# A two-layer encoder on one core: two projections in 512-column blocks, a new order of the projection stage, and three smaller moves

## The chip, the cores and the metric

The kernel runs on one core of a Trainium2 chip. The metric is device time in microseconds (us); lower is better. A core has five engines that run their own instruction streams and wait for one another on semaphores: PE (TensorE, matrix products), DVE (VectorE), ACT (ScalarE), POOL (GpSimd) and SP (SyncE, which here issues all DMA transfers). PE writes its results to PSUM; this kernel divides PSUM into seven shared banks of 128x512 values and one more for sums.

## The reference

Two equal layers work on x of 2048 tokens by 1024 features, in float32.

```
h    = rmsnorm(x, pre_g)
proj = h @ W_in                        # 1024 x 2816
u_a, v_a, g_a, q, k, v, g_b = split(proj, [512, 512, 512, 512, 128, 128, 512])
# group A, chunks of 128 positions, 8 channel groups of 64
z    = W_s (128x128 per group) @ layernorm(v_a) + b
y_a  = u_a * z * silu(g_a)
# group B, 8 query heads, 2 kv heads, head size 64, all tokens attend to all
q, k = axial_rope(rmsnorm(q)), axial_rope(rmsnorm(k))
y_b  = softmax(q k^T / 8) v * silu(g_b)
out  = concat(y_a, y_b) @ W_out
x    = x + rmsnorm(out, post_g)
```

## The kernel before

**Precision.** A projection multiplies in three passes: each operand is split into a high part (rounded to the matrix engine's float32 form) and a low rest, and high x high, high x low and low x high are added up in PSUM. With 8 slices of 128 features, one output tile takes 24 matmuls. Weights are loaded as `w_raw`, then split: ACT copies the high part `w_hi`, DVE subtracts to get `w_lo` (L268), in pieces of 128x1024 values.

**Stages.** A layer has a projection stage and an attention stage. The projection stage runs over two halves; a half has two groups of 512 tokens, a group four token tiles of 128. `hT` holds a group's normalised, transposed activations. For each half `run` goes, weight block by weight block, over both groups:

1. keys and values (`do_kv`), and the first four query heads (`do_q`, block 0);
2. Q1, the last four query heads (`do_q`, block 1);
3. VA, the mixed values v_a: two blocks of 256 columns into one PSUM bank, then `do_va`: layer norm on DVE (L424 to L429), a split by ACT and POOL (`fl`, L436), and 16 "mixes" per group, each three matmuls with the spatial weights `ws` and two DVE steps into `fb` with the bias `zbias` (L448), the result stored to `z_d`;
4. GB, the second gate g_b: two blocks of 256 columns, a tanh on ACT, one DVE step (L476), a store to `gb_d`;
5. the first gate and u_a, four times 128 + 128 columns (`do_gate`), here with the weights as the stationary operand and 512 activations streaming (`proj_ch`).

With tokens as the stationary operand (`proj_tok`), a matmul streams 256 weight columns. `norm_rope` is the work on a group of queries: squares on ACT, a sum (L351), a reciprocal root by ten small steps, a multiply (L358), t1 on POOL (L360), t2 on DVE (L363) and their sum `fc` (L365); PE then transposes `fc` and the result goes to `q_d`.

**Order.** PE's instructions stand in program order. Work that has to be slipped in between projections (transposes, mixes, the first row maxima) is put in a list `bg` with a delay in ticks; a tick is 8 matmuls of 256 columns or 4 of 512, and takes up to two due jobs. `spatial_weights` makes the transposed weights `wsT` and `zbias` in such jobs. The other engines' instructions in the projection stage are ordered by a scheduler; in the attention stage they stand in program order too. SP issues its DMAs in order, and an issue that waits holds all behind it.

**Row maxima.** Attention needs the row maximum of every score before the softmax. They come from a separate cheap product: for one unit (a group and a head) 16 matmuls `pmax` from `q_m`, each followed by a DVE maximum into `mx` (L683), then `m_neg` over four of them (`max_row`), then `stack_max`, in which PE transposes m_neg and the rows go to `m_d`. The first eight units run as jobs during GB and the first gate in the layer's second half (`last_jobs`, after `scale_v`, which finds the values' maximum); the others during attention, spread over its key tiles.

**Attention.** For each unit, 16 key tiles of 128: two matmuls `sp`, two exponentials on ACT (`p_parts`, `p_f`), a subtraction on POOL or DVE (`p_parts`), products `po` and `sums`. Between them PE does the output product `pout` of the group before (`fill`). Behind each finished token tile a list `post_queue` holds small steps: a reciprocal root, two adds `o_t`, a store, and in layer 0 also a norm for the next layer. In each key tile the loop takes steps from it; when a last part begins, the queue is emptied at once.

Of the kernel before, what the change touches and what calls it, by code (L numbers as in the profile page):

```python
# [9 lines left out]
F32 = mybir.dt.float32  # L10
# [9 lines left out]
P = 128  # L20
# [5 lines left out]
HD = 64  # L26
# [12 lines left out]
def encoder(ctx: ExitStack, tc, x, w_in, w_out, pre_g, post_g, ln_a_g, ln_a_b,  # L39
# [31 lines left out]
    def ps_t(name):  # L71
        return psum.tile([P, GRP], F32, name=name, tag="ps", bufs=7)
# [102 lines left out]
    class Project:  # L175
# [39 lines left out]
        def spatial_weights(self):  # L215
            l = self.l
            self.lng = lay.tile([P, 4], F32, name="lng")
            nc.sync.dma_start(self.lng, ln_a_g[l].rearrange("(t p) -> p t", p=P))
            self.zbias = lay.tile([P, 4, P], F32, name="zbias")
            wsT = row_t("wsT")  # L220
            for hf in range(2):
                raw = f_t("fa")
                nc.sync.dma_start(raw.rearrange("p (g j) -> p g j", g=4),
                                  spatial_w[l, 4 * hf:4 * hf + 4].rearrange("g i j -> i g j"))
                hi = f_t("fh", dt=F32R)
                lo = f_t("fl", dt=F32R)

                def t(hf=hf, raw=raw, hi=hi, lo=lo):
                    ps = ps_t("pt")
                    for g in range(4):  # L230
                        PE.transpose(ps[:, g * P:(g + 1) * P], raw[:, g * P:(g + 1) * P], ident)
                    sl = slice(hf * GRP, (hf + 1) * GRP)
                    nc.vector.tensor_copy(wsT[:, sl], ps)
                    nc.scalar.copy(hi, wsT[:, sl])
                    nc.gpsimd.tensor_tensor(lo, wsT[:, sl], hi.bitcast(F32), ALU.subtract)
                    nc.sync.dma_start(ws_d[:, 0, sl], hi.bitcast(F32))
                    nc.sync.dma_start(ws_d[:, 1, sl], lo.bitcast(F32))
                bg.add(WS_DELAY + 2 * hf, t)
            lnb = f_t("fb")
            nc.sync.dma_start(lnb, ln_a_b[l].partition_broadcast(P))  # L240
            sb = row_t("sb_row", (1, D))
            nc.sync.dma_start(sb, spatial_b[l:l + 1].rearrange("o g i -> o (g i)"))
            for c in range(4):
                def b(c=c):
                    ps = ps_t("pt")
                    PE.matmul(ps[:, 0:2 * P], lnb[:, c * P:(c + 1) * P], wsT[:, 2 * c * P:(2 * c + 2) * P],
                              start=True, stop=False)
                    PE.matmul(ps[:, 0:2 * P], ones1, sb[:, 2 * c * P:(2 * c + 2) * P], start=False, stop=True)
                    nc.vector.tensor_copy(self.zbias[0:HD, c, :], ps[0:HD, 0:P])
                    nc.vector.tensor_copy(self.zbias[HD:P, c, :], ps[HD:P, P:2 * P])  # L250
                bg.add(WS_DELAY + 8 + 2 * c, b)

        def load_w(self, cols):
# [7 lines left out]
        def split_w(self, raw, n=4):  # L261

            hi = w_t([P, ND, WB], "w_hi")
            lo = w_t([P, ND, WB], "w_lo")
            for d in range(0, ND, n):
                sl = slice(d, d + n)
                nc.scalar.copy(hi[:, sl], raw[:, sl])  # L267
                nc.vector.tensor_tensor(lo[:, sl], raw[:, sl], hi.bitcast(F32)[:, sl], ALU.subtract)  # L268
            return hi, lo

        def hT_jobs(self, g, tail=False):

# [41 lines left out]
        def proj_tok(self, hT, j, w, ps=None, c0=0):  # L314
            if ps is None:
                ps = ps_t("pp")
            n = 0
            for a, b in PASSES:
                for d in range(ND):
                    PE.matmul(ps[:, c0:c0 + WB], hT[d // 4][:, a, d % 4, j * P:(j + 1) * P], w[b][:, d, :],  # L320
                              start=(n == 0), stop=(n == 3 * ND - 1))
                    n += 1
                bg.tick()
            return ps

        def proj_ch(self, hT, w, c0):
# [142 lines left out]
            nc.sync.dma_start(y_d[g][:, c, 0], hi.bitcast(F32))  # L469
            nc.sync.dma_start(y_d[g][:, c, 1], lo.bitcast(F32))  # L470

        def do_gb(self, g, banks, b):
            for i, ps in enumerate(banks):
                th = f_t("fa")
                nc.scalar.activation(th, ps, AF.Tanh, scale=0.5)
                nc.vector.scalar_tensor_tensor(th, th, 1.0, ps, ALU.add, ALU.mult)  # L476
                nc.sync.dma_start(gb_d[g][:, 2 * i:2 * i + 2, b * WB:(b + 1) * WB],
                                  th.rearrange("p (t e) -> p t e", t=2))

        def scale_v(self):  # L480

# [39 lines left out]
        def run(self, kv, first, last_jobs, first_wo):  # L521
# [5 lines left out]
            for n, gs in enumerate(halves):  # L527
# [13 lines left out]
                for i, g in enumerate(gs):  # L541
                    if i == 0:
                        for f in self.stores:
                            f()
                        self.stores = []
                    if i == len(gs) - 1:
                        raw = self.load_w([C_Q + WB])
                    self.do_kv(g, self.banked(hTs[g], w_kv))
                    if i == len(gs) - 1:
                        w_next = self.split_w(raw)  # L550
                        raw = self.load_w([C_VA])
                    self.do_q(g, self.banked(hTs[g], w), 0)
                if n == 0:
                    self.spatial_weights()
                w = w_next
                for i, g in enumerate(gs):
                    self.do_q(g, self.banked(hTs[g], w), 1)
                    if i == 0:
                        w_next = self.split_w(raw)
                w = w_next  # L560
                raw = self.load_w([C_VA + WB])
# [3 lines left out]
                w = [w, self.split_w(raw)]  # L565
                raw = self.load_w([C_GB])
                for g in gs:
                    vs = []
                    for j in range(TPG):
                        ps = self.proj_tok(hTs[g], j, w[0])  # L570
                        self.proj_tok(hTs[g], j, w[1], ps, WB)
                        v = f_t("fv")
                        nc.scalar.copy(v, ps)
                        vs.append(v)
                    self.do_va(g, vs, ws)
                w = self.split_w(raw)
                blocks = [[C_GB + WB]] + [[C_GA + c * P, C_U + c * P] for c in range(4)]
# [5 lines left out]
                for b in range(2):  # L583
                    raw = self.load_w(blocks.pop(0))
                    for i, g in enumerate(gs):
                        self.do_gb(g, self.banked(hTs[g], w), b)
                        if i == 0:
                            w_next = self.split_w(raw)
                    w = w_next
# [39 lines left out]
    def attend(l, kv, nxt):  # L629
# [25 lines left out]
        def at(k, f):  # L655
            later.setdefault(k, []).append(f)
# [33 lines left out]
        def stack_max(u, pe, act, dve):  # L690
            s = state[u]
            qb, h = units[u]
            ps = ps_t("t2")
            pe.transpose(ps[0:TPG, 0:P], s.m, ident)
            for i in range(2):
                rows = small.tile([TPG, P], F16, name="m_rows", bufs=4)
                if i == 0:
                    hi = rows
                    act.activation(rows, ps[0:TPG, 0:P], AF.Copy, bias=EXP_SHIFT)
                else:  # L700
                    dve.scalar_tensor_tensor(rows, ps[0:TPG, 0:P], EXP_SHIFT, hi, ALU.add, ALU.subtract)
                nc.sync.dma_start(m_d[qb][h, i].rearrange("(t p) -> t p", p=P), rows)
# [341 lines left out]
        for u in range(pre, len(units)):  # L1044
            k0 = (u - pre) * span
            if k0 >= 8:
                at(k0 - 8, lambda u=u: load_qm(u))
            for n in range(steps):
                at(k0 + n * span // steps, lambda u=u, n=n: max_step(u, n, PE, DVE))
            at(k0 + span + 1, lambda u=u: max_row(u, DVE))  # L1050
            at(k0 + span + 3, lambda u=u: stack_max(u, PE, ACT, DVE))

        def load_gb(u):
            qb, h = units[u]
# [37 lines left out]
        for k in range(end + 4):  # L1092
            if k < total:
# [10 lines left out]
                ACT.activation(p_f(k), sp, AF.Exp)  # L1104
                if not dve_share(k):
                    sub_lo(k, POOL)
            for _ in range(2):
                if post_queue:
                    post_queue.pop(0)()
            kb = k - 1  # L1110
            if 0 <= kb < total and dve_share(kb):
                sub_lo(kb, DVE)
# [119 lines left out]
```

## Time and profile before

| | |
|---|---|
| median of 3 runs | 2775.79 us (2775.23 to 2775.82) |
| profiled execution | 2771.47 us, of it 2769.3 us span |
| projection and attention, layer 0 | about 0 to 629 and 629 to 1382 us |
| projection and attention, layer 1 | about 1382 to 1992 and 1992 to 2769 us |
| PE busy in these four stretches | 595, 736, 597, 749 us |
| DVE busy in them | 461, 496, 452, 488 us |
| mean granted clock of PE | 0.992 |

How to read it: the page gives busy time and count of each engine; records of matmuls overlap, so the mean of one (290 ns at 256 columns) is longer than the distance to the next. A group's row ends with the idle time ahead of its instructions and what released them; a row of waits has total, times and longest; a timeline row has the start, the length of a run of equal instructions with their number, and in brackets the idle time before it. A row of a window has, after the window and its length, busy time and count of PE, PEld (the weight loads), DVE, ACT and POOL, then the granted clock, the DMA share and GB/s. Nearly all instructions of the attention stage, and PE's everywhere, carry L84, the line of a helper, so they are told apart by tile names.

### The profile page before, as it was taken

What the parts mean: (1) busy time and instruction counts of PE and PEld (TensorE: products, weight loads), DVE (VectorE), ACT (ScalarE), POOL (GpSimd) and SP (SyncE); (2) the same over time, 40 slices, a digit from 0 to 9 for tenths busy, and PEclk for the clock granted to TensorE, in tenths of its full rate; (3) what the DMA queues carried; (4) which work ended last, traced back from release to release, by engine and by line L of the source; (5) the groups of instructions that cost most, each with busy time, mean ns of one, the idle gap of its engine ahead of it and who ended that gap; (6) DMA issues with size and microseconds to landing.
All of it is one profiled execution on the core that took longest, in us unless ns stands there. A gap on an engine that the chain in (4) does not pass through costs nothing.

```text
span 2769.3 us, 48428 instructions
## 1 busy us (share of the span) xinstructions
PE 2677.1 (97%) x18230; PEld 1782.0 (64%) x18230; DVE 1896.8 (68%) x3796; ACT 1522.7 (55%) x3005; POOL 1287.0 (46%) x1080
## 2 busy tenths in 40 slices
PE   7999999999999999999999999999999999999997
PEld 6898899764444444444589989997644444444444
DVE  8862688876666776776487528888766666666664
ACT  4221432117887787787732214221288877778774
POOL 1210122007786676776632101210277767667765
PEclk9999999999999999999999999999999999999999
DMA  4424522322222232222354334333322222221313
GB/s 143 146 81 127 165 76 81 112 63 89 89 71 81 75 98 79 82 80 80 110 179 138 115 114 134 88 92 98 94 64 72 82 70 73 81 76 47 112 46 129
DMA packets 275310, 265.31 MB, mean 96 GB/s; under 512 B 19202, under 2 KB 233346, under 8 KB 275076
## 3 DMA queue, kind: packets, MB, share of 16 engines
q1 hardware_dynamic: 275076, 262.22, 30.2%
q8 instruction: 143, 2.34, 0.3%
q14 instruction: 91, 0.75, 0.1%
HBM read 177.09 MB, written 85.07 MB: 95 GB/s over the span
## 4 chain that ended last, share of the span: by engine, by line
PE 77%; DVE 11%; ACT 5%; DMA 3%; issue 2%; POOL 1%; SPq 0%; DVEq 0%; POOLq 0%; ACTq 0%
PE pp L84 27%; PE sp L84 14%; PE po L84 11%; PE pout L84 11%; PE pmax L84 7%; PE sums L84 4%; PE pt L84 2%; DVE fc L363 2%; ACT p_parts L84 2%; ACT p_f L84 2%; DMA w_raw<-in_w_in_dram 1%; DVE mx L84 1%; DVE o_t L84 1%; DVE w_lo L268 1%; ACT w_hi L267 1%
## 5 line engine op out<-in xcount | busy, mean ns | idle before, releaser
L84 POOL TENSOR_TENSOR p_parts<-p_f,p_parts 128x512 f16<-128x512 f32 x872 | 1034.9, 1205 | 404.2 <-ACT p_f L84 304.3
L84 ACT ACTIVATE p_parts<-sp 128x512 f16<-128x512 f32 x1024 | 630.0, 615 | 296.5 <-PE sp L84 289.8
L84 DVE TENSOR_REDUCE mx<-pmax 128x1 f32<-128x512 f32 x768 | 513.0, 681 | 211.9 <-PE pmax L84 209.9
L84 PE MATMUL pout<-wo,y_t 128*128 128x512 f32 x1488 | 657.1, 506 | 0.7 <-ACT p_f L84 0.3
L84 PE MATMUL po<-p_parts,v_st 128*32 128x512 f16 (+1 forms) x3072 | 639.2, 383 | 0.2
L84 ACT ACTIVATE p_f<-sp 128x512 f32<-128x512 f32 x1024 | 632.0, 617 | 0.0
L84 PE MATMUL pp<-w_hi,hT 128*128 128x256 f32 x3584 | 502.5, 290 | 16.1 <-DVE hT L310 9.7
L84 PEld LDWEIGHTS pp<-w_hi,hT 128*128 128x128 f32 x3584 | 462.0, 194 | 21.8 <-DVE hT L310 10.9
L84 PE MATMUL sp<-q_st,k_t 128*128 128x512 f16 x1024 | 390.2, 381 | 8.3 <-DVE mx L84 5.5
L84 PE MATMUL pmax<-k_t,q_m 128*128 128x512 f16 x1024 | 389.7, 382 | 7.6 <-DVE mx L84 3.2
L84 PEld LDWEIGHTS <-v_st 128*32 128x32 f16 (+1 forms) x3072 | 193.7, 96 | 309.5 <-issue 253.0
L84 PE MATMUL sp<-q,k_t 66*128 66x512 f16 x1024 | 391.0, 382 | 0.0
L84 PEld LDWEIGHTS pout<-wo,y_t 128*128 128x128 f32 x1488 | 281.3, 190 | 128.4 <-issue 8.7
L84 PEld LDWEIGHTS <-k_t 128*128 128x128 f16 (+1 forms) x2048 | 191.5, 99 | 187.7 <-issue 74.4
L468 POOL TENSOR_TENSOR fl<-fa,fh 128x512 fp32r<-128x512 f32 x32 | 43.1, 1346 | 533.3 <-ACT fh L467 489.2
L84 PE MATMUL pp<-hT,w_hi 128*128 128x512 f32 x1024 | 271.7, 413 | 0.0
L84 PE MATMUL pp<-w_lo,hT 128*128 128x256 f32 x1792 | 262.6, 290 | 0.0
L84 PE MATMUL sums<-p_parts,one_h 128*32 128x512 f16 x2048 | 242.3, 380 | 0.0
L84 PEld LDWEIGHTS pp<-w_lo,hT 128*128 128x128 f32 x1792 | 235.5, 194 | 0.9
L84 PEld LDWEIGHTS pp<-hT,w_hi 128*128 128x128 f32 x1024 | 193.4, 190 | 35.3
L683 DVE TENSOR_REDUCE mx<-pmax 128x1 f32<-128x512 f32 x256 | 172.6, 687 | 49.1 <-PE pmax L84 47.5
L84 PEld LDWEIGHTS <-q_m 128*128 128x128 f16 x1024 | 99.8, 98 | 140.2 <-issue 42.1
(161 smaller groups left out, 2790.9 us busy)
## 6 DMA issues: line engine op xcount, KB each, us to landing
w_raw<-in_w_in_dram SPq DMA_DIRECT2D x28, 1024.0 KB
y_t<-y_d SPq DMA_DIRECT2D x56, 512.0 KB
w_raw<-in_w_in_dram SPq DMA_DIRECT2D x32, 512.0 KB
x_t<-in_x_dram SPq DMA_DIRECT2D x16, 512.0 KB
z_d<-fb SPq DMA_DIRECT2D x32, 256.0 KB
gb_d<-fa SPq DMA_DIRECT2D x32, 256.0 KB
fb<-z_d SPq DMA_DIRECT2D x32, 256.0 KB
y_d<-fh SPq DMA_DIRECT2D x32, 256.0 KB
```

The lines of the kernel that those rows point to most:

```text
L84: return tc.keep_in_program_order(call(*args, **kw))
L267: nc.scalar.copy(hi[:, sl], raw[:, sl])
L268: nc.vector.tensor_tensor(lo[:, sl], raw[:, sl], hi.bitcast(F32)[:, sl], ALU.subtract)
L363: nc.vector.tensor_tensor(t2[:, :, :, lo:lo + 16], qn[:, :, :, hi:hi + 16], tbi[:, :, 1:2, lo:lo + 16].broadcast_to([P, 2, n, 16]), ALU.mult)
L468: nc.gpsimd.tensor_tensor(lo, th, hi.bitcast(F32), ALU.subtract)
L683: dve.tensor_reduce(s.mx[:, j, c:c + 1], ps, AX.X, ALU.max)
```

## The change

The layer's order becomes: keys and first queries, VA, Q1, GB, first gate. VA and GB use weights of 512 columns: `load_wide` loads two tiles of four feature slices each, `split_wide` splits them on ACT and DVE, and `proj_wide` multiplies 512 columns at once, with a tick every 4 matmuls. `do_gb` now stores one token tile at a time. `spatial_weights` is called ahead of the first group's queries, not after both groups'; its copies out of PSUM move from DVE to ACT. The second half of a 256-column weight block's low part is made on GpSimd. In attention `stack_max` comes two key tiles later, and the loop takes one step from `post_queue` in a key tile, not two.

```diff
 spatial_weights:
-                    nc.vector.tensor_copy(wsT[:, sl], ps)
+                    nc.scalar.copy(wsT[:, sl], ps)
...
-                    nc.vector.tensor_copy(self.zbias[0:HD, c, :], ps[0:HD, 0:P])
-                    nc.vector.tensor_copy(self.zbias[HD:P, c, :], ps[HD:P, P:2 * P])
+                    nc.scalar.copy(self.zbias[0:HD, c, :], ps[0:HD, 0:P])
+                    nc.scalar.copy(self.zbias[HD:P, c, :], ps[HD:P, P:2 * P])
 split_w:
-                nc.vector.tensor_tensor(lo[:, sl], raw[:, sl], hi.bitcast(F32)[:, sl], ALU.subtract)
+                engine = nc.gpsimd if n == 4 and d else nc.vector
+                engine.tensor_tensor(lo[:, sl], raw[:, sl], hi.bitcast(F32)[:, sl], ALU.subtract)
+        def load_wide(self, c):
+            raws = [w_t([P, ND // 2, 2 * WB], "w_raw", F32) for _ in range(2)]
+            for q, raw in enumerate(raws):
+                nc.sync.dma_start(raw, w_in[self.l, q * GRP:(q + 1) * GRP, c:c + 2 * WB]
+                                  .rearrange("(d p) e -> p d e", p=P))
+            return raws
+        def split_wide(self, raws):
+            parts = [], []
+            for raw in raws:
+                hi, lo = [w_t([P, ND // 2, 2 * WB], name) for name in ("w_hi", "w_lo")]
+                for d in range(0, ND // 2, 2):
+                    sl = slice(d, d + 2)
+                    nc.scalar.copy(hi[:, sl], raw[:, sl])
+                    nc.vector.tensor_tensor(lo[:, sl], raw[:, sl], hi.bitcast(F32)[:, sl], ALU.subtract)
...
+        def proj_wide(self, hT, j, w):
+            ps = ps_t("pp")
+            n = 0
+            for a, b in PASSES:
+                for d in range(ND):
+                    PE.matmul(ps, hT[d // 4][:, a, d % 4, j * P:(j + 1) * P], w[b][d // 4][:, d % 4, :],
+                              start=(n == 0), stop=(n == 3 * ND - 1))
+                    n += 1
+                    if n % 4 == 0:
+                        bg.tick()
+            return ps
 do_gb:
-                nc.sync.dma_start(gb_d[g][:, 2 * i:2 * i + 2, b * WB:(b + 1) * WB],
-                                  th.rearrange("p (t e) -> p t e", t=2))
+            nc.sync.dma_start(gb_d[g][:, j], th)
 run, order of a half:
+                    if n == 0 and i == 0:
+                        self.spatial_weights()
...
-                for i, g in enumerate(gs):
-                    self.do_q(g, self.banked(hTs[g], w), 1)
...
-                        ps = self.proj_tok(hTs[g], j, w[0])
-                        self.proj_tok(hTs[g], j, w[1], ps, WB)
+                        ps = self.proj_wide(hTs[g], j, w)
...
+                    if i == 0:
+                        w_next = self.split_w(raw)
+                w = w_next
+                raws = self.load_wide(C_GB)
+                for i, g in enumerate(gs):
+                    self.do_q(g, self.banked(hTs[g], w), 1)
+                    if i == 0:
+                        w_next = self.split_wide(raws)
...
+                for i, g in enumerate(gs):
+                    for j in range(TPG):
+                        self.do_gb(g, j, self.proj_wide(hTs[g], j, w))
 attend:
-            at(k0 + span + 3, lambda u=u: stack_max(u, PE, ACT, DVE))
+            at(k0 + span + 5, lambda u=u: stack_max(u, PE, ACT, DVE))
...
-            for _ in range(2):
-                if post_queue:
-                    post_queue.pop(0)()
+            if post_queue:
+                post_queue.pop(0)()
```

Three pieces of the engines' order show what moves; the line numbers behind the change are those of the changed file. First DVE in layer 0's second half, from the last norm of the values to the first maxima `mx`. Before (`rs_y`, `rs_t` are the reciprocal root, `fv` the normed values):

```order
L448 SCALAR_TENSOR_TENSOR fb<-pt,lng,zbias 64x128
L124 SCALAR_TENSOR_TENSOR rs_t<-rs_t,ms_v 128x4
L448 SCALAR_TENSOR_TENSOR fb<-pt,lng,zbias 64x128
L125 SCALAR_TENSOR_TENSOR rs_y<-rs_t,rs_y 128x4
L429 TENSOR_SCALAR fv<-fv,mv_v,rs_y 128x512 x4
L683 TENSOR_REDUCE mx<-pmax 128x1 x2
L493 TENSOR_REDUCE v_row<-pt 1x1
```

And with the change, the end of the second group's Q1:

```order
L125 SCALAR_TENSOR_TENSOR rs_y<-rs_t,rs_y 128x16
L392 TENSOR_TENSOR fc<-pp,rs_y 128x512
L397 TENSOR_TENSOR fc<-fc,fa 128x8x16 x4
L392 TENSOR_TENSOR fc<-pp,rs_y 128x512
L399 TENSOR_TENSOR fc<-fc 128x512
L397 TENSOR_TENSOR fc<-fc,fa 128x8x16 x4
L399 TENSOR_TENSOR fc<-fc 128x512
L445 TENSOR_TENSOR fl<-pt,fh 128x512
L714 TENSOR_REDUCE mx<-pmax 128x1
L213 TENSOR_SCALAR gain_q<-gain_q,g_exp 128x128
L714 TENSOR_REDUCE mx<-pmax 128x1
```

The first maximum, which stood behind the norm of the values, now stands behind the last rotation of queries, and a step on the next layer's `gain_q` follows it. Second, DVE some 20 rows ahead of that, with the change, where the mixes of the second group meet the first group's Q1:

```order
L392 TENSOR_TENSOR fc<-pp,rs_y 128x512
L399 TENSOR_TENSOR fc<-fc 128x512
L397 TENSOR_TENSOR fc<-fc,fa 128x8x16 x4
L482 SCALAR_TENSOR_TENSOR fb<-pt,lng,zbias 64x128
L399 TENSOR_TENSOR fc<-fc 128x512
L482 SCALAR_TENSOR_TENSOR fb<-pt,lng,zbias 64x128 x15
L269 TENSOR_TENSOR w_lo<-w_raw,w_hi 128x1024
```

Fifteen steps of mixes, which before had only weights and norms beside them, come in one piece behind a rotation. Third, SP at the first `q_m` of layer 0. Before:

```order
L415 DMA q_d_115<-fl 64x2x256 x2
L452 DMA z_d_142<-fb 512x1x128 x3
L257 DMA w_raw<-in_w_in_dram 128x8x128
L665 DMA q_m<-q_d_112 128x512
L257 DMA w_raw<-in_w_in_dram 128x8x128
L452 DMA z_d_142<-fb 512x1x128
```

And with the change:

```order
L486 DMA z_d_143<-fb 512x1x128 x3
L374 DMA fa<-in_rope_dram 128x4x128
L257 DMA w_raw<-in_w_in_dram 128x8x128 x2
L675 DMA wo_raw<-in_w_out_dram 128x1024
L486 DMA z_d_143<-fb 512x1x128
L675 DMA wo_raw<-in_w_out_dram 128x1024
L197 DMA gain_q<-in_q_norm_g_dram 128x64
L696 DMA q_m<-q_d_112 128x512
```

`z_d_142` and `z_d_143` are the third and fourth group's mixed values. `q_m` stood behind three stores of the third group's; it now stands behind the last store of the fourth group's.

More of the change, by code (lines that the diff above doesn't have):

```diff
@@ L267, in split_w @@
                 nc.scalar.copy(hi[:, sl], raw[:, sl])
-                nc.vector.tensor_tensor(lo[:, sl], raw[:, sl], hi.bitcast(F32)[:, sl], ALU.subtract)
+                engine = nc.gpsimd if n == 4 and d else nc.vector
+                engine.tensor_tensor(lo[:, sl], raw[:, sl], hi.bitcast(F32)[:, sl], ALU.subtract)
             return hi, lo
+        def load_wide(self, c):
[12 more added lines that the diff above has]
+                    nc.vector.tensor_tensor(lo[:, sl], raw[:, sl], hi.bitcast(F32)[:, sl], ALU.subtract)
+                parts[0].append(hi)
+                parts[1].append(lo)
+            return parts
         def hT_jobs(self, g, tail=False):
@@ L470, in do_gate, with do_gb @@
             nc.sync.dma_start(y_d[g][:, c, 1], lo.bitcast(F32))
[L472 to L476, printed above, removed]
-                nc.sync.dma_start(gb_d[g][:, 2 * i:2 * i + 2, b * WB:(b + 1) * WB],
-                                  th.rearrange("p (t e) -> p t e", t=2))
+        def do_gb(self, g, j, ps):
+            th = f_t("fa")
+            nc.scalar.activation(th, ps, AF.Tanh, scale=0.5)
+            nc.vector.scalar_tensor_tensor(th, th, 1.0, ps, ALU.add, ALU.mult)
+            nc.sync.dma_start(gb_d[g][:, j], th)
         def scale_v(self):
@@ L546, in run @@
                     if i == len(gs) - 1:
-                        raw = self.load_w([C_Q + WB])
+                        raws = self.load_wide(C_VA)
                     self.do_kv(g, self.banked(hTs[g], w_kv))
+                    if n == 0 and i == 0:
+                        self.spatial_weights()
                     if i == len(gs) - 1:
-                        w_next = self.split_w(raw)
-                        raw = self.load_w([C_VA])
+                        w_next = self.split_wide(raws)
                     self.do_q(g, self.banked(hTs[g], w), 0)
-                if n == 0:
-                    self.spatial_weights()
                 w = w_next
-                for i, g in enumerate(gs):
-                    self.do_q(g, self.banked(hTs[g], w), 1)
[L558 to L561, printed above, removed]
                 ws = [row_t("ws", dt=F32R) for _ in range(2)]
@@ L564, in run @@
                     nc.sync.dma_start(ws[i].bitcast(F32), ws_d[:, i])
-                w = [w, self.split_w(raw)]
-                raw = self.load_w([C_GB])
-                for g in gs:
+                raw = self.load_w([C_Q + WB])
+                for i, g in enumerate(gs):
                     vs = []
                     for j in range(TPG):
-                        ps = self.proj_tok(hTs[g], j, w[0])
-                        self.proj_tok(hTs[g], j, w[1], ps, WB)
+                        ps = self.proj_wide(hTs[g], j, w)
                         v = f_t("fv")
@@ L575, in run @@
                     self.do_va(g, vs, ws)
-                w = self.split_w(raw)
-                blocks = [[C_GB + WB]] + [[C_GA + c * P, C_U + c * P] for c in range(4)]
+                    if i == 0:
[5 more added lines that the diff above has]
+                    if i == 0:
+                        w_next = self.split_wide(raws)
+                w = w_next
+                blocks = [[C_GA + c * P, C_U + c * P] for c in range(4)]
                 if n + 1 < len(halves):
@@ L582, in run @@
                     last_jobs()
[L583 to L589, printed above, removed]
+                raw = self.load_w(blocks.pop(0))
+                for i, g in enumerate(gs):
+                    for j in range(TPG):
+                        self.do_gb(g, j, self.proj_wide(hTs[g], j, w))
+                    if i == 0:
+                        w_next = self.split_w(raw)
+                w = w_next
                 for c in range(4):
```

## The prediction

> **What bounds the kernel now.** I read the page's head first, then the groups by shape, then the waits of the matmul engine (PE), then timelines around each wait.
>
> ```profile
> span 2769.3 us, 48428 instructions
> PE 2677.1 (97%) x18230; PEld 1782.0 (64%) x18230; DVE 1896.8 (68%) x3796; ACT 1522.7 (55%) x3005; POOL 1287.0 (46%) x1080
> L84 PE MATMUL pp<-w_hi,hT 128*128 128x256 f32 x3584 | 502.5, 290 | 16.1 <-DVE hT L310 9.7 <-DVE zbias L250 4.5 <-DVE k_t L396 1.2
> L84 PE MATMUL pp<-w_lo,hT 128*128 128x256 f32 x1792 | 262.6, 290 | 0.0
> ```
>
> PE is the bound, so time is lost only where it runs small matmuls or waits. Its 97% is no measure of speed, because records overlap: the price of a matmul is the distance between starts. The timeline gives it for both widths, with one of PE's waits.
>
> ```profile
> 183.29 0.39 PE L84 MATMUL pt<-ws,fl 128*128 128x256 f32 x1 [1.29 <-POOL fl L436]
> 183.51 1.12 PE L84 MATMUL pp<-w_hi,hT 128*128 128x256 f32 x8
> 184.47 0.40 PE L84 MATMUL pt<-ws,fh 128*128 128x256 f32 x2
> 255.38 1.98 PE L84 MATMUL pp<-hT,w_lo 128*128 128x512 f32 x8
> 257.20 3.79 PE L84 MATMUL pp<-hT,w_hi 128*128 128x512 f32 x16
> 260.82 1.52 PE L84 MATMUL pp<-hT,w_lo 128*128 128x512 f32 x6
> ```
>
> Eight of 256 columns take 184.47 - 183.51 = 0.96 us, 120 ns each; sixteen of 512 columns take 3.62 us, 226 ns (eight before them 227). What PE waits for, longest first where the change touches it (total, times, longest):
>
> ```profile
> PE t L84 <- DVE m_neg L84: 6.3, 9, 1.1
> PE sp L84 <- DVE mx L84: 5.5, 6, 1.9
> PE pp L84 <- DVE zbias L250: 4.5, 2, 2.5
> PE pt L84 <- DVE fc L365: 3.9, 4, 3.0
> PE pt L84 <- POOL fl L436: 2.6, 2, 1.3
> PE pmax L84 <- DVE fb L448: 1.6, 2, 0.8
> PE t L84 <- ACT p_f L84: 1.3, 1, 1.3
> PE pt L84 <- DVE wsT L233: 0.7, 1, 0.7
> 123.23 2.05 PE L84 MATMUL pp<-w_hi,hT 128*128 128x256 f32 x8 [2.47 <-DVE zbias L250]
> 125.08 1.76 PE L84 MATMUL pp<-w_lo,hT 128*128 128x256 f32 x8
> 126.68 0.59 PE L84 MATMUL pt<-wsT,fb 128*128 128x256 f32 x2
> 392.27 0.67 PE L84 MATMUL pt<-ident,fc 128*128 128x128 f32 x4 [3.00 <-DVE fc L365]
> ```
>
> After the wait at 123 us, sixteen matmuls take 126.68 - 123.23 = 3.45 us instead of 1.92: a long wait costs about 1.5 us more in slower matmuls.
>
> **Width (sum: -20.4 us).** Mixed values and second gate are 3072 matmuls of 256 columns in two layers; they become 1536 of 512. Each pair cost 240 ns, its successor 226.7: 13.3 ns x 1536 = 20.4 us. They lie on PE's path, nothing hides them. The one assumption is that 226.7, measured with the activations streaming, holds with the weights streaming; both stationary tiles are 128x128. Ends: 0 and 20.4; I take the rows. The Trainium skill (TensorE: Matmul & The Clock Gate, "Back-to-back issue gap") gives a lone warm matmul columns / 2.4 + 2.5 ns, which leaves only 2.5 ns to save on each removed matmul, an estimate of 3.8 us in place of 20.4. The trace disagrees, 120 ns standing where that rule gives 109.
>
> **Order in the first half of each layer (-9.3, +3.4).** The mixed values now come straight after keys and first queries; the second queries, Q1, follow them. The spatial weights are prepared earlier and leave PSUM on ACT. So the waits on zbias (4.5, and 1.5 of slow matmuls behind the longer one), on the transposed weights wsT (0.7) and on POOL's fl (2.6), all in the first halves, should go: 9.3. What hides the copies is ACT's idle time (it is busy 16.13 of 58 us in the last row below); if ACT is late, the waits stay: ends 0 and -9.3. But DVE now normalises and rotates Q1's first group ahead of fifteen mix steps. What that costs DVE:
>
> ```profile
> L351 DVE TENSOR_REDUCE ms_q<-fb 128x8 f32<-128x512 f32 x32 | 20.6, 674 | 6.2 <-ACT fb L350 6.2
> L363 DVE TENSOR_TENSOR fc<-fc,fa 128x128 f32<-128x128 f32 x128 | 69.0, 598 | 10.1 <-POOL fa L342 9.2
> L365 DVE TENSOR_TENSOR fc<-fc 128x512 f32<-128x512 f32 x32 | 22.4, 699 | 0.0
> L358 DVE TENSOR_TENSOR fc<-pp,rs_y 128x512 f32<-128x512 f32 x32 | 21.9, 685 | 0.5
> L125 DVE SCALAR_TENSOR_TENSOR rs_y<-rs_t,rs_y 128x16 f32<-128x16 f32 x48 | 9.4, 196 | 1.5
> L424 DVE BATCH_NORM_STATS2 st_v<-fv 128x6 f32<-128x512 f32 x32 | 22.0, 687 | 17.9 <-ACT fv L573 17.6
> L429 DVE TENSOR_SCALAR fv<-fv,mv_v,rs_y 128x512 f32<-128x512 f32 x32 | 19.3, 666 | 0.3
> L448 DVE SCALAR_TENSOR_TENSOR fb<-pt,lng,zbias 64x128 f32<-64x128 f32 x256 | 89.3, 349 | 45.6 <-PE pt L84 42.4
> L268 DVE TENSOR_TENSOR w_lo<-w_raw,w_hi 128x1024 fp32r<-128x1024 f32 x84 | 104.4, 1256 | 18.8 <-ACT w_hi L267 17.6 <-PE pp L84 0.6
> 440.00:498.00 58.00, 57.85 (x463) 55.87 (x462) 51.42 (x118) 16.13 (x24) 7.40 (x5) 1.00 0.32 94
> ```
>
> One rotation of a group is 2 x 0.67 + 11 x 0.2 + 2 x (0.685 + 69.0/32 + 0.70) = 10.6 us. Meanwhile PE goes on through mixes: of seven PSUM banks two hold projections, five take mixes, some 6 ticks of 0.96 and 5 mixes of 0.36 = 7.6 us. So PE waits 10.6 - 7.6 = 3.0 at most, 0 if it meets DVE later; I take 1.7, between: 1.7 x 2 = +3.4 here and the same again in the second halves.
>
> **Second half of each layer (+3.4, +5.8, +18.3, -1.6).** Two places. First, the transposes of the first queries (the wait of 3.00 above; the other three of 3.9 are 0.9 together). DVE reaches them about 2 us later (one more weight split of 1.256 and the value maxima ahead of them), PE some 0.7 earlier. I take +2.3 in layer 0, +3.5 with slower matmuls in layer 1: +5.8; ends 0 and +8. Second, the first pass of maxima (pmax), which starts in the second gate's fourth tick. In the row above DVE is already at 51.42 of 58 us, and PE loses nothing. Now Q1's rotation stands in between: from the end of the mixed values PE needs 192 x 0.12 (Q1) + 16 x 0.36 (mixes) + 4 x 0.91 and a few transposes, about 34 us; DVE has 32 x 0.349 = 11.2 (mixes), 10.6 (rotation), 5 x 1.256 = 6.3 (weights), 3 x 0.69 + 4 x 0.67 + 11 x 0.2 = 6.9 (norm of the values): 35. The rotation of the second group (10.6) comes next, still ahead of the first maximum, when PE has only five banks, 5 x 1.13 us, of lead: a wait of 10.6 + 35 - 34 - 5.7 = 6. The load of q_m gives about the same from another side: on SP it now stands behind the last store of mixed values, whose last mix DVE ends near 36; SP issues that store, a weight load and a gain load, and q_m has to land: some 5 us, an estimate that no row bounds better, so near 41 against PE's 35 to 36, some 5.4. The two lie beside each other, not after one another. I take 5.4, 0.8 for a query transpose behind, in layer 0 another 2.7 for a gain load that DVE waits for between two maxima, and 1.6 slow clock each: 10.5 + 7.8 = +18.3; ends 0 and +32. The waits of pmax on fb (1.6) go.
>
> **Weight parts on GpSimd (0).** 26 halves of 1.256 us leave DVE. GpSimd's nearest price is 1.205 us for half as many elements, so 2.4 us each, and there is a catch:
>
> ```profile
> L84 POOL TENSOR_TENSOR p_parts<-p_f,p_parts 128x512 f16<-128x512 f32 x872 | 1034.9, 1205 | 404.2 <-ACT p_f L84 304.3 <-PE sp L84 59.2 <-PE pmax L84 26.2
> 121.48 1.26 POOL L342 TENSOR_TENSOR fa<-fa,gain_q 128x512 f32<-128x512 f32 x1 [6.09 <-issue]
> 121.50 1.26 DVE L125 SCALAR_TENSOR_TENSOR rs_y<-rs_t,rs_y 128x16 f32<-128x16 f32 x1
> ```
>
> A DVE step of 0.196 us lasts 1.26, exactly as long as POOL's beside it. So a half on POOL may hold DVE for 2.4 to save it 1.26. Only the piece in the mixed-value stage of the second halves falls where DVE sets the pace: -2.5 to +2.3, taken as 0. The rule of the Trainium skill (SBUF — State Buffer, "Who interferes with whom") says the same: a DVE instruction with two SBUF inputs and a GpSimd instruction that reads SBUF exclude each other for a whole instruction. By that rule this term is +2.3. Loads and gate stores keep their bytes; DMA queues are under half busy, 0.
>
> **Attention (-11.1).** The row maxima's transposes wait for m_neg and once for p_f, 6.3 + 1.3 = 7.6 us, each at most 1.3. Two key tiles later is 2.2 us later (1.12 each below), so all should go: -7.6. Post steps come one by one:
>
> ```profile
> 951.51 3.03 DVE L84 SCALAR_TENSOR_TENSOR o_t<-o_t,rs_o,x_r 128x512 f32<-128x512 f32 x2
> 708.71 0.58 PE L84 MATMUL pout<-wo,y_t 128*128 128x512 f32 x1
> 709.83 0.58 PE L84 MATMUL pout<-wo,y_t 128*128 128x512 f32 x1
> 955.20 0.38 PE L84 MATMUL sp<-q_st,k_t 128*128 128x512 f16 x1 [1.90 <-DVE mx L84]
> ```
>
> Two adds back to back, 3.03 us, delay maxima, and PE waits 1.90. Of the 5.5 us on mx in PE's waits, with slow matmuls behind the longest as at 123 us, I take 5 as saved (ends 0 and 8), and give 1.5 back for steps that are flushed at the end: a token tile's 24 steps at one per tile last 24 of its 32 tiles, so its rows come free in time but later.
>
> **Sum.** -20.4 - 9.3 + 3.4 + 3.4 + 5.8 + 18.3 - 1.6 - 11.1 = -11.5 us. The profiled execution took 2771.5 (span 2769.3 and 2.2 around it), 4.3 below the median of 2775.8. So 2760.0 for a profiled one, 2764.3 for the median.
>
> **Rivals.**
> *The second halves stay smooth.* The scheduler's order of DVE is fixed, but PE's lead in banks may carry it, as it does at 440 to 498 us. Then +18.3 falls away: -29.8, 2746.
> *Slower.* DVE's rotations ahead of the first maxima. POOL's products hold DVE as at 121.50, so 10.6 grows, and every us that DVE is later there is a us of PE in each layer. It decides when the second-half wait passes 9.2 + (11.5 + 5.5)/2 = 17.7 us a layer; at 20 it is -11.5 + 21.6 = +10.1: 2785.9. For it: DVE at 51.42 of 58. Against: both estimates above say 5 to 6.
> *Attention gives nothing*, since its waits move on to the next late DVE step: -0.4, 2775.4. For it: DVE is the releaser of nearly all these waits.
> *Width gives a fifth.* If a 512-column matmul with the weights streaming took 237.5 ns, almost twice the 120, and not the 226.7 of streaming activations, the term is 3.8 us and the sum +5.1: 2780.9. The sixteen matmuls at 226 ns speak against it. It is what the TensorE page of the Trainium skill, cited above, would give.
>
> **Chances.** A measurement of this kernel tells 0.2%, 5.5 us. Forecast (-5.5 to -20) 0.46; smooth second halves 0.21; attention gives nothing 0.14; width a fifth 0.04; slower 0.15. So faster 0.67, same 0.18, slower 0.15. The range, 2742 to 2782, leaves out the far half of the smooth case and most of the slower one; the forecast's own is 2756 to 2770.
>
> **What will show it.** Distances of 227 ns at the new 512-column matmuls; no zbias and no m_neg row among PE's waits; a new wait of about 5 us before the first pmax of each layer, on q_m or mx; mixes waiting on fb 1 to 3 us in each half. If the first pmax waits 15 us, or ACT's copies are late, the prediction is wrong.

## The result: 0.37% slower, with the width's gain in it

The changed kernel took 2784.03 us (median of 7 runs, 2781.47 to 2784.29), the kernel before 2775.23 (7 runs, 2771.66 to 2776.34): a ratio, as recorded, of 1.0037, 95% interval 1.0027 to 1.0047 (the medians alone stand 8.8 us apart, 0.32%). Forecast were 2764.3 and at most 2782. The profiled spans are 2779.7 and 2769.3, so the traces stand 10.4 us apart, and all differences between stretches below are of these two.

A line of the page after the change, the engines' busy time:

```profile
PE 2667.1 (96%) x16694; PEld 1693.7 (61%) x16694; DVE 1861.5 (67%) x3750; ACT 1526.5 (55%) x3025; POOL 1350.7 (49%) x1106
```

PE issues 1536 matmuls fewer, as it should, and DVE is busy 35 us less; both have become idle longer. Cutting both traces at the first and last gate product, the first score product and the first projection product of layer 1 shows where. These marks are exact; the bounds of layer 1 in the first table (about 1382 and 1992) lie 24 and 4 us ahead of them:

| stretch | before, us | after, us | difference | by the prediction's terms |
|---|---|---|---|---|
| layer 0, start to first half's gate | 226.3 | 217.6 | -8.8 | -9.4 |
| layer 0, second half to its gate | 205.2 | 221.8 | +16.6 | +8.6 |
| layer 0, attention, to next projection | 777.2 | 771.7 | -5.5 | -5.5 |
| layer 1, to first half's gate | 192.8 | 191.5 | -1.3 | -6.7 |
| layer 1, second half to its gate | 200.0 | 212.9 | +12.9 | +7.1 |
| layer 1, attention to the end | 773.4 | 770.0 | -3.4 | -5.6 |

The gates take 88.3 and 108.6 us in both. The terms of the width (5.1 in each half), the order and attention are shared out to their stretches (attention's by halves); the six differences make +10.5. What PE waits for after the change:

```profile
PE pmax L84 <- DMA q_m<-q_d: 16.2, 2, 8.6
PE pt L84 <- DVE fb L482: 11.0, 4, 2.8
PE pt L84 <- DVE fc L399: 8.4, 2, 6.5
PE pmax L84 <- DVE mx L84: 7.3, 11, 2.3
PE pt L84 <- POOL fl L470: 3.6, 4, 0.9
PE pt L84 <- ACT fh L469: 2.2, 4, 0.5
PE pt L84 <- DVE fl L445: 1.4, 1, 1.4
```

No row for zbias and none for m_neg is left. In their place stand the load of `q_m`, the mixes behind `fb`, and longer waits on `fc`. The width itself gives what was forecast where wide matmuls follow one another (timeline of PE in layer 0):

```profile
123.06 1.99 PE L84 MATMUL pp<-w_hi,hT 128*128 128x512 f32 x8
124.88 0.40 PE L84 MATMUL pt<-ws,fh 128*128 128x256 f32 x2
```

Eight matmuls of 512 columns take 124.88 - 123.06 = 1.82 us, 227 ns each, with the weights streaming. But many of the new matmuls have a job slipped in after every four. With mixes between them, a few rows earlier:

```profile
121.77 1.09 PE L84 MATMUL pp<-w_hi,hT 128*128 128x512 f32 x4
122.70 0.40 PE L84 MATMUL pt<-ws,fh 128*128 128x256 f32 x2
```

And in the second gate, from one row maximum to the next, first before, then after the change:

```profile
506.71 0.39 PE L84 MATMUL pmax<-k_t,q_m 128*128 128x512 f16 x1
507.89 0.39 PE L84 MATMUL pmax<-k_t,q_m 128*128 128x512 f16 x1
```

```profile
507.74 0.39 PE L84 MATMUL pmax<-k_t,q_m 128*128 128x512 f16 x1
508.90 0.39 PE L84 MATMUL pmax<-k_t,q_m 128*128 128x512 f16 x1
```

Four wide matmuls take 0.93 us there, against 0.96 for eight narrow ones, and with a maximum 1.16 against 1.18: some 8 and 5 ns are saved on each, not 13.3.

The largest wait, in layer 0's second half, as PE and SP saw it:

```profile
471.72 0.61 PE L84 MATMUL pmax<-k_t,q_m 128*128 128x512 f16 x1 [8.61 <-DMA q_m<-q_d]
```

```profile
465.01 0.53 SPq L486 DMA_DIRECT2D z_d<-fb  x1
465.63 0.57 SPq L675 DMA_DIRECT2D wo_raw<-in_w_out_dram  x1
466.30 0.40 SPq L197 DMA_DIRECT2D gain_q<-in_q_norm_g_dram  x1
466.75 0.44 SPq L696 DMA_DIRECT2D q_m<-q_d  x1
```

`q_m`'s data had been in memory for long. Its issue stands behind the store of the last mix, which SP could start at 465.01, and comes at 466.75; five us later it has landed, while PE had been ready since 463. The second large wait has the same form one step further back:

```profile
372.80 1.24 SPq L449 DMA_DIRECT2D q_d<-fh  x2
...
378.76 0.60 SPq L374 DMA_DIRECT2D fa<-in_rope_dram  x1
```

```profile
SPq L276 <- DVE w_lo L269: 10.6, 1, 10.6
SPq L276 <- POOL w_lo L269: 2.2, 1, 2.2
```

```profile
381.90 1.26 POOL L376 TENSOR_TENSOR fa<-fa,gain_q 128x512 f32<-128x512 f32 x1 [10.97 <-DMA fa<-in_rope_dram]
```

```profile
386.50 1.09 PE L84 MATMUL pt<-ident,fc 128*128 128x128 f32 x4 [6.46 <-DVE fc L399]
```

PE waits 6.46 us for queries that DVE rotates late, because POOL had no rotation table: its load was issued at 378.76, behind a weight load that waited 10.6 us for a free buffer, then 2.2 more for the weight part that GpSimd makes, and behind eight stores of queries that began at 372.80. The page names DVE; the cause is two steps behind it, on SP. The window 386 to 392 us also shows what such a wait costs beyond itself: PE's granted clock is 0.72 there (0.98 in the 80 us ahead).

```profile
386.00:392.00 6.00, 5.50 (x23) 4.65 (x24) 5.48 (x12) 1.66 (x3) 1.48 (x1) 0.72 0.14 34
```

### The profile page after: what moved, and what is told of

It is laid out like the page before. It is cut to its first block, busy times and chain, and to the rows that moved or that the text cites. A ratio compares the mean times of both kernels' runs of the same rounds, so it can differ in the third digit from the quotient of the medians.

```text
span 2779.7 us, 45408 instructions
## 1 busy us (share of the span) xinstructions
PE 2667.1 (96%) x16694; PEld 1693.7 (61%) x16694; DVE 1861.5 (67%) x3750; ACT 1526.5 (55%) x3025; POOL 1350.7 (49%) x1106
## 5 line engine op out<-in xcount | busy, mean ns | idle before, releaser
L84 PE MATMUL pp<-w_hi,hT 128*128 128x256 f32 (+1 forms) x2560 | 491.2, 339 | 7.9 <-DVE hT L331 7.2
L84 PEld LDWEIGHTS pp<-w_hi,hT 128*128 128x128 f32 x2560 | 392.9, 196 | 45.9 <-DVE hT L331 8.4
L84 PE MATMUL pmax<-k_t,q_m 128*128 128x512 f16 x1024 | 391.1, 382 | 28.4 <-DMA q_m<-q_d 16.2
L84 PE MATMUL pp<-w_lo,hT 128*128 128x256 f32 (+1 forms) x1280 | 248.2, 334 | 0.0
L269 POOL TENSOR_TENSOR w_lo<-w_raw,w_hi 128x1024 fp32r<-128x1024 f32 x26 | 64.5, 2482 | 337.1 <-ACT w_hi L267 292.1
L84 PEld LDWEIGHTS pp<-w_lo,hT 128*128 128x128 f32 x1280 | 194.2, 192 | 18.3 <-issue 1.6
```

What stands on the lines that cost most here:

```text
L84: return tc.keep_in_program_order(call(*args, **kw))
L269: engine.tensor_tensor(lo[:, sl], raw[:, sl], hi.bitcast(F32)[:, sl], ALU.subtract)
```

## The experiments

Twelve kernels ran, in three groups. Each was timed against the kernel before on its own chip, whose median moved from 2772.9 to 2777.2, so kernels of different groups are compared by their ratio to it. "us against before" is (ratio - 1) x 2775.

| kernel | median, us | ratio (95% interval) | us against before |
|---|---|---|---|
| the change | 2784.03 | 1.0037 (1.0027 to 1.0047) | +10.3 |
| e1 new order only | 2813.94 | 1.0142 (1.0121 to 1.0162) | +39.4 |
| e2 attention only | 2766.48 | 0.9973 (0.9963 to 0.9982) | -7.5 |
| e3 change, loads off SP | 2762.60 | 0.9958 (0.9943 to 0.9973) | -11.7 |
| e4 change, weight parts on DVE | 2788.70 | 1.0051 (1.0037 to 1.0066) | +14.2 |
| e5 change, q_m early | 2776.39 | 1.0013 (1.0003 to 1.0022) | +3.6 |
| e6 wide mixed values, old order | 2781.77 | 1.0033 (1.0020 to 1.0046) | +9.2 |
| e7 change, short rotation | 2767.19 | 0.9979 (0.9969 to 0.9988) | -5.8 |
| e8 new order in first halves only | 2759.03 | 0.9949 (0.9934 to 0.9963) | -14.2 |
| e9 e6, gain steps late | 2765.93 | 0.9963 (0.9949 to 0.9977) | -10.3 |
| e10 e8, gain steps late | 2753.66 | 0.9919 (0.9904 to 0.9934) | -22.5 |
| e11 change, loads off SP, gain late | 2756.09 | 0.9928 (0.9913 to 0.9943) | -20.0 |
| e12 e10, tables off SP | 2748.00 | 0.9895 (0.9880 to 0.9910) | -29.1 |

**e1, the new order alone.** The edit to the kernel before; the first two lines tell the order in words, the others are code, cut short:

```diff
-  kv, q0 | Q1 | VA block 0, 1 | GB block 0 | GB block 1 | gate
+  kv, q0 | VA block 0, 1 | Q1 | GB blocks 0 and 1, group by group | gate
+                    if n == 0 and i == 0:
+                        self.spatial_weights()
```

> The kernel before with only the new order (keys, first queries, mixed values, second queries, second gate; spatial weights prepared earlier), all blocks 256 columns wide, all weight parts and copies on DVE, attention as before. Theory 1 (the order makes the loss: loads stand late on SP and queries' rotations ahead of the maxima): the change's own result (+8.8 us) without the width's -20.4 and attention's -8.8, so +38 us, about 2813; the second halves grow by 20 us each, the waits on q_m and on the queries' transposes are there. Theory 2 (the order is harmless, the new waits come from the shorter stages of wide blocks and from the weight parts on GpSimd): within 10 us of before, no wait on q_m over 2 us.

It came out at 2813.94, +39.4. PE's waits in its trace:

```profile
PE pmax L84 <- DMA q_m<-q_d: 20.6, 2, 11.1
PE pt L84 <- DVE fb L448: 11.0, 4, 2.8
PE pt L84 <- DVE fc L365: 6.3, 2, 4.1
```

The same three waits as after the whole change, with blocks of 256 columns and no weight part on GpSimd: they belong to the order.

**e2, the attention edits alone.** The diff is the section "attend" of the change.

> The kernel before with only the two attention edits (row maxima transposed two key tiles later, one post step per key tile). The traces show the attention stages 5.5 and 3.3 us shorter after the change: if these edits did that by themselves, -8.8 us (2766), no wait on m_neg. If the waits only move on to the next late DVE step, -2 to 0.

2766.48, -7.5 (-10.3 to -5.0). Row maxima no longer delay transposes, but PE's waits on `mx` did not go: before they were 5.5 on sp and 3.2 on pmax, here

```profile
PE pmax L84 <- DVE mx L84: 7.4, 11, 2.3
PE sp L84 <- DVE mx L84: 0.9, 4, 0.3
```

8.7 us in 9 waits, the longest 1.9, became 8.3 us in 15, the longest 2.3: they moved from sp to pmax. So the 7.6 us of waits ahead of the row maxima's transposes (m_neg, and once p_f) went, and the slower post queue took next to nothing from the waits on `mx`.

**e3, the loads off SP** (the code is shortened).

```diff
-            nc.sync.dma_start(cs..., rope[...])
+            nc.scalar.dma_start(cs..., rope[...])
...
                 raws = self.load_wide(C_GB)
+                if n + 1 == len(halves):
+                    last_jobs.early()        # load_qm(0, nc.scalar)
```

> The changed kernel with the rotation tables' loads issued by ACT instead of SP, and the first q_m loaded at the start of the second queries, by ACT too. Theory 1a (loads wait in SP's order): the wait for the first queries' transposes (6.5 us in layer 0) falls to 1 or less, the first pmax no longer waits for q_m (8.6 + 7.6 us) and PE runs five banks ahead, then waits some 4 to 5 us for the first maximum, which DVE makes after the rotation: -5 -1 - 2 x 4 = -14 us, about 2770. Theory 1b (DVE's rotations alone set the pace): q_m's wait turns into an equal wait on mx, -3 us at most.

2762.60: 22 us faster than the change in ratio, with no instruction of PE, DVE or POOL taken away. The second halves are 13.2 and 8.7 us shorter than in the change's trace, layer 0's first half 6.1 longer. The wait on q_m is gone, the first maxima's waits are the first two rows, and a new one stands in layer 0's first half:

```profile
PE pmax L84 <- DVE fl L445: 3.6, 2, 1.8
PE pmax L84 <- DVE fc L392: 2.3, 2, 1.1
PE pt L84 <- DVE k_t L430: 3.2, 1, 3.2
```

It ends behind four rotation steps on DVE that last 5.21 us, 1.99 in the bank before. POOL works beside them, and its product for the keys' table, whose load ACT has issued, is one of its pieces:

```profile
67.86 5.21 DVE L397 TENSOR_TENSOR fc<-fc,fa 128x128 f32<-128x128 f32 x4
```

```profile
69.05 2.60 POOL L235 TENSOR_TENSOR fl<-wsT,fh 128x512 fp32r<-128x512 f32 x2
71.62 1.30 POOL L376 TENSOR_TENSOR fa<-fa,gain_k 128x512 f32<-128x512 f32 x1
```

**e4, all weight parts on DVE.**

```diff
-                engine = nc.gpsimd if n == 4 and d else nc.vector
+                engine = nc.vector
```

> The changed kernel with all weight parts on DVE again. If a part on GpSimd holds DVE for its whole 2.5 us (a step of 0.41 us lasted 2.62 beside it): the wait of 1.4 us on keys' transposes in layer 0 goes, those on POOL's fl shrink, -1 to -4 us. If GpSimd relieves DVE where it sets the pace: +2 to +5 us.

2788.70, +3.9 against the change by ratios. The intervals of the two overlap, so the difference is not clear of the noise. The wait on q_m is longer, and the wait of 1.4 on the keys' transposes is gone, as the first theory said:

```profile
PE pmax L84 <- DMA q_m<-q_d: 21.1, 2, 11.0
```

16.2 became 21.1, but not because the last mix came later against PE: SP issues its store 1.0 us after PE is ready in both layers, 1.9 in the change. What grew is the way behind it. In layer 0 SP now issues two weight loads between that store and q_m, and q_m's own issue waits 2.0 us for a step of POOL:

```profile
467.36 0.53 SPq L486 DMA_DIRECT2D z_d<-fb  x1
468.74 1.07 SPq L257 DMA_DIRECT2D w_raw<-in_w_in_dram  x2
469.90 3.71 SPq L696 DMA_DIRECT2D q_m<-q_d  x1
```

The lock of DVE by POOL that I feared is there, in the changed kernel's layer 0:

```profile
368.23 2.70 POOL L269 TENSOR_TENSOR w_lo<-w_raw,w_hi 128x1024 fp32r<-128x1024 f32 x1 [1.17 <-ACT w_hi L267]
368.60 2.62 DVE L399 TENSOR_TENSOR fc<-fc 128x256 f32<-128x256 f32 x1
366.04 0.41 DVE L399 TENSOR_TENSOR fc<-fc 128x256 f32<-128x256 f32 x1
```

An add of 0.41 us lasts 2.62 beside it. The Trainium skill (SBUF — State Buffer, "Who interferes with whom") states the exclusion, and the trace agrees. So the time lies where the second theory put it, but a relief of DVE is not shown: the edit also moved loads in SP's order.

**e5, the first q_m early, by SP.** The `last_jobs.early()` of e3 with `load_qm(0)`, tables as in the change.

> The changed kernel with only the first unit's q_m loaded earlier in the program (at the start of the second queries, still by SP). Loads by ACT gained 21 us together; this splits the sum. Theory 1 (each late load costs by itself): the waits on q_m (8.6 and 7.6 us) become some 4.5 us on mx in each layer, the wait of 6.5 on the first queries' transposes stays: -10 to -14 us, about 2772. If the tables' loads carried the gain (DVE gets its work earlier), -3 us at most.

2776.39, 6.7 us less than the change by ratios, 3.6 by the spans: between the two numbers of the expectation. The wait on q_m is gone, but PE runs into DVE's rotation right after. The waits in layer 0, where the change had one of 8.6 and one of 1.3:

```profile
470.68 0.27 PE L84 MATMUL pt<-ident,v_top 128*1 128x128 f32 x1 [0.46 <-DVE mx L716]
471.78 1.20 PE L84 MATMUL pp<-w_hi,hT 128*128 128x512 f32 x4 [0.83 <-DVE mx L716]
475.06 0.38 PE L84 MATMUL pmax<-k_t,q_m 128*128 128x512 f16 x1 [0.94 <-DVE fc L392]
478.14 0.61 PE L84 MATMUL pmax<-k_t,q_m 128*128 128x512 f16 x1 [2.70 <-DVE fl L445]
```

0.46 + 0.83 + 0.94 + 2.70 = 4.9 us: as the prediction said, two waits lay beside each other, and half of the loss is DVE's. In this half PE waits 3.7 us less than after the change, but its mean granted clock is no better, 0.96 in both, and the half is only 0.5 us shorter. The other 15 us of e3 (its ratio against this one) came with the tables, and with ACT instead of SP as the issuer of q_m.

**e6, the width without the order.** Before, with `load_wide`, `split_wide` and `proj_wide` for the mixed values alone.

> The kernel before with only the mixed values in one 512-column block; the order, the second gate in two blocks, copies, weight parts and attention as before (both wide projections in the old order do not fit the weight buffers). The width alone: 768 matmuls fewer, 13.3 ns each, -10.2 us, about 2764. If shorter stages leave DVE behind, new waits on fc or fb eat it: -5 to 0.

2781.77: slower than before by 9.2, and no fc or fb wait of the kind expected explains it. In layer 0's second half PE waits 9.4 us on fc:

```profile
PE pt L84 <- DVE fc L398: 10.6, 4, 9.4
```

And DVE, which should make it, stands:

```profile
426.83 0.28 DVE L213 TENSOR_SCALAR gain_q<-gain_q,g_exp 128x128 f32<-128x128 f32 x1 [10.77 <-DMA gain_q<-in_q_norm_g_dram]
```

```profile
417.77 0.94 SPq L201 DMA_DIRECT2D gain_q<-in_q_norm_g_dram  x2
```

The scheduler has put a step of the *next* layer, the scaling of its query gains, in the middle of a rotation of this one; the last of the gains' three loads is issued near 418.3, and the step starts 8.6 us later.

**e7, a shorter rotation of the second queries.** It leaves out the t2 products (the code is shortened).

```diff
-                        nc.vector.tensor_tensor(t2...)     # four per bank
-                nc.vector.tensor_tensor(qn, t1, t2, ALU.add)
+                nc.vector.tensor_tensor(qn, t1, t1 if short else t2, ALU.add)
```

> The changed kernel without the t2 products of the second queries' rotation (it adds t1 to itself; four DVE steps of 0.54 us fewer in each bank). It leaves out part of the computation. If the mixes' waits on fb (2.8 us in each half) come from DVE being in the rotation, 4.3 us less of it takes them away: -2.8 x 4 and slow matmuls of 0.8 x 4 = -14 us, about 2770, while the waits on q_m stay. If they come from the PSUM banks or from POOL's fl, they stay and the time is within 4 us.

2767.19, 16 us less than the change by ratios. The mixes' wait shrinks from 11.0 to

```profile
PE pt L84 <- DVE fb L482: 2.6, 4, 0.7
PE pmax L84 <- DMA q_m<-q_d: 15.9, 2, 8.2
```

while q_m's stays: the mixes wait for the rotation, and the two waits are separate.

**e8, the new order in the first halves only.** In the second halves Q1 comes ahead of the mixed values again, these 512 wide, the second gate in two blocks.

> The changed kernel with its new order in the first halves only; the second halves take the old order (second queries ahead of the mixed values), with the mixed values 512 columns wide and the second gate in two blocks. From the traces: first halves as after the change (-8.8 and -1.4 against before), second halves as before less 2.6 each for the width, attention -8.8: -24 us, about 2751. If the loss of the second halves comes from the wide mixed values or the weight parts on GpSimd and not from the order, it stays above 2765.

2759.03, -14.2 and not -24. Part of the missing 10 is again a gain step of the next layer in layer 0's second half:

```profile
362.46 0.29 DVE L212 TENSOR_SCALAR gain_k<-gain_k,g_inv 128x128 f32<-128x128 f32 x1 [4.86 <-DMA gain_k<-in_k_norm_g_dram]
```

**e9 and e10, the gain steps kept in their layer.** In `gains`, the eight DVE steps are kept in program order, so that layer 1's come behind layer 0's attention; e9 is e6 with this, e10 is e8.

```diff
-            nc.vector.tensor_scalar(self.gain_q, self.gain_q, e, HD ** -0.5, ALU.mult, ALU.mult)
+            DVE.tensor_scalar(self.gain_q, self.gain_q, e, HD ** -0.5, ALU.mult, ALU.mult)
```

> The kernel before with the mixed values in one 512-column block, old order (+9 us when run alone), and the next layer's gain steps kept in program order on DVE, so that they come at that layer's start and not between rotations of the layer before. Theory 1 (DVE stood 10.8 us at the gain_q step for a load that SP issued late; PE waited 9.4 for the transposes behind it and 4.9 at keys' copies): those two waits and the slow matmuls behind them go, -9.4 - 4.9 - 2 = -16: some 2766, and the width's gain of 10.2 shows against before. Theory 2 (the width itself makes DVE late): the waits stay at another step, time above 2778.

> The kernel with the new order in the first halves and the old one in the second halves (2759), plus the next layer's gain steps in program order. DVE stood 4.9 us at the gain_k step in layer 0's second half and PE 3.6 behind it: -4 to -6 us, 2754. If DVE is late there anyway: within 1 us.

2765.93 and 2753.66. e9 is 10.3 us faster than before (6.4 to 14.2), against 768 x 13.3 ns = 10.2: the width pays as soon as nothing lies in DVE's way. Whether it pays in full is not shown. The profiled spans stand only 5.3 us apart (2769.3 and 2764.0), and if every four of the 768 were broken as above they would save 8 ns each, 6 us, which the interval nearly holds too. Late gain steps can be little of it: in the kernel before, DVE waits 1.3 us at them. e6's wait of 9.4 on fc is 1.1 at the longest now.

```profile
PE pt L84 <- DVE fc L398: 2.8, 4, 1.1
```

**e11 and e12, all together.** e11 is the change with q_m early and the second halves' tables loaded by ACT, and the gain steps kept; e12 is e10 with the tables of the second halves loaded by ACT.

> The changed kernel with q_m and the rotation tables loaded by ACT, the tables only in the second halves (in the first they brought a wait of 3.3 us on keys), and the gain steps in program order. Against the 2762.6 of the version with all tables on ACT: -3.3 - 1.5 for the first half, -2 for the gain step: some 2756. If the tables' loads in the first halves were part of the gain, 2763 or more.

> New order in the first halves, old in the second, gain steps in program order, and the rotation tables of the second halves loaded by ACT. The waits on fc in the second halves (2.6 + 1.2 and 2.2 us, with 2.1 on its first step) come from late tables: -6 to -8 against the version without ACT's loads, and -4 for the gain step: some 2748, the fastest version. If ACT's queue delays the tables as SP's did, the same as without it.

2756.09 and 2748.00: e12 is 1.05% faster than the kernel before (0.9 to 1.2%) and has the lowest median of all; its interval just touches that of e10. Its waits of any size on the projection stage's new places are the mixes' of the first halves, 2.8 us each:

```profile
PE pt L84 <- DVE fb L483: 5.5, 2, 2.8
```

## Why the prediction was wrong

**Right in kind.** The waits on zbias and m_neg that go, the place of the new waits (the first queries' transposes, the mixes, the first pmax), q_m behind the last store of mixes on SP, and 227 ns at wide matmuls in a row. The rival of the Trainium skill's rule (TensorE: Matmul & The Clock Gate, "Back-to-back issue gap"), that widening would save 2.5 ns a matmul, fell: the trace shows 227 ns against 240 in a row and 5 to 8 saved in the worst places.

**The step that failed is the sum of the second halves.** It was put at +18.3 + 5.8 + 3.4 - 1.6, less 10.2 for the width: +15.7 for both layers, against +29.5 measured. A stretch of a trace can be split into PE's waits, the slow clock (half of the time outside waits in which the profile has the granted clock at one half, when a matmul takes nearly twice its time), and the rest, matmuls at full pace. This split is an estimate from the two traces; of layer 1's +3.5 for the transposes it counts 1.2 as slow matmuls.

| second halves of both layers, after less before | measured, us | by the prediction's terms |
|---|---|---|
| PE's waits | +28.7 | +21.5 |
| slow clock | +6.8 | +4.4 |
| the rest: the width | -6.0 | -10.2 |

So the waits were sized too low by 7 us, the slow clock by 2 and the width too high by 4. The terms, by the trace after:

- q_m: 5.4 said, 8.6 and 7.6 measured. The prediction had the last mix done when PE is ready, and some 5 us from there to the data. In layer 0 SP issues that mix's store 1.9 us after PE is ready (465.01 and 463.1), and from there to the first pmax it is 6.7: 1.7 until q_m is issued and 5.0 until it has landed. Behind it 0.8 was said, and 2.7 more in layer 0 for the gain load; 1.3 came there.
- The first queries' transposes: +2.3 and +3.5 said. 6.5 now for 3.0 in layer 0 (+3.5), with 1.4 more on keys' transposes, behind POOL's weight part; 1.95 for 0.31 in layer 1. The reason given, more DVE work, was not it: the table's load was late, and with the tables off SP (e3) 1.6 is left in all.
- The mixes: 1.7 in each half said, 2.8 measured. It was a midpoint between 0 and 3.0; the order listed all fifteen mix steps behind the rotation, which spoke for the upper end. Behind three of the four waits come slow matmuls that I had put at nothing: in layer 0's second half the next eight take 1.71 us in place of 0.96.

```profile
451.79 1.91 PE L84 MATMUL pp<-w_hi,hT 128*128 128x256 f32 x8
453.50 0.63 PE L84 MATMUL pt<-ws,fh 128*128 128x256 f32 x2
```

- POOL's fl and ACT's fh, ahead of the first mix of each half: I had them go (-2.6). They are 3.6 + 2.2 = 5.8 us, in all four halves.

**The width, -20.4, was too large by about 6.** The same split puts the rest at -14.7 over the four halves (-4.2, -3.0, -4.5, -3.0). The price of 13.3 ns came from rows without a job between them, and the jobs between every four matmuls were given no price.

**Layer 1's first half** missed by 5.4: 1.4 of it are fl and fh, 1.1 the mixes, and by the same split 2.3 the slow clock and 0.6 the width.

**Attention** was put at -11.1 and gave -7.5 alone in e2 and -8.9 in the traces. Its 7.6 for m_neg came; the 5 for `mx` did not, since those waits only moved to pmax. On that part the rival "attention gives nothing" was right.

**Weight parts on GpSimd** were put at 0. e4 is 3.9 us slower without them, with overlapping intervals and SP's order changed, so their worth stays open.

**The slower rival** had a chance of 0.15 and named DVE's rotation as the mechanism. The loss is on its side of zero, but only half of it is that: e5 shows 4.9 us of DVE behind q_m, e7 the mixes; the rest is loads that SP issues late, which e3 gave back by 22 us without touching DVE's work. The range was too short by 2 us at the top. The unsure terms were sized one by one at middles, though all of them lie in the same stretch, where one engine's lateness feeds the next: DVE's mix, SP's store, q_m, PE.

**The ledger.** Order alone +39.4 (e1), width -20.4 by the price of a row or -14.7 by the split, attention -7.5 (e2), weight parts -3.9 (e4): +7.6 or +13.3, against +10.3 measured. e1's interval alone is 11 us wide, so the sum closes but cannot choose between the two. Copies on ACT were not run alone; what is left of their cost or gain lies in that difference. Also open is the gain step's share in the changed kernel: DVE stood 4.7 us there in layer 0 and PE 1.3 behind it; it was not taken away alone.

## What to carry to other kernels

A wait that names a compute engine is followed back until something is found that was not busy; here the trail ended twice on SP, at a load whose data were ready and whose issue stood behind transfers that waited for steps of another stage. When a stage is moved, read the in-order queue of the transfers as closely as that of the engines: a load that gates the bound belongs ahead of every store that has to wait, or in another queue. And an instruction of a later phase that a scheduler slips in early can hold an engine for its own late load, so a measured loss may come from neither part of an edit (e6: +9.2, the same edit in e9: -10.3).

## What was not expected of the hardware

- Loads of 16 KB of gains, the last issued near 418.3 us in e6, were followed by the step that needed them at 426.8, 8.6 us later; q_m's 128 KB took 5.0 (466.75 to 471.7). Why is not shown.
- A DVE add was held by POOL for 2.62 us in place of 0.41, and four rotation steps for 5.21 in place of 1.99.
- Short waits of PE can bring a slow clock, and need not. Before the change each of two waits of 1.9 us on `mx` (955.2 and 1149.8) is followed by 3.4 us at half clock; after it, the wait of 2.74 us at 165.6 is followed by none, and the next eight matmuls take 0.96 us. After the wait of 6.5 us the granted clock was 0.72 over six us.
